# A batch pipeline with bf16 transposes, 8 KB loads of four consecutive rows, and a PSUM copy that restores the row order

## The chip, the cores and the metric

The kernel runs on one core of a Trainium2 chip. The metric is device time in microseconds, the median of several runs. A profile covers one execution; its span is some 2 us shorter than the timed figure (98.6 against 100.73 us for the kernel before). A run over 1.5% above the fastest of the same kernel counts as slow, and ratios use fast runs alone.

## The reference

```python
batch, m, k, n = 16, 512, 512, 512            # x: (16,512,512) fp32, weight: (512,512) fp32
y = scale * np.matmul(x, weight)              # scale = 0.125
y = np.where(mask == 1, y, -1e9)              # mask: strictly lower triangle
y_exp = np.exp(y - np.max(y, axis=-1, keepdims=True))
return y_exp / np.sum(y_exp, axis=-1, keepdims=True)
```

The mask is causal: rows 128·mt to 128·mt+127 need only the first 128·(mt+1) columns. Every kernel here uses that, so a tile of 128 output rows must hold consecutive rows. x is read (16.8 MB), the result written (16.8 MB).

## The kernel before

An item is 128 rows of one batch, 64 items in all. x is loaded one batch (1 MB) at a time with 2 KB rows, transposed in fp32 on PE, cast to bf16 on the way out of PSUM, multiplied, exponentiated with a row sum, and scaled.

```python
xf_pool = tile_pool(name="xf", bufs=3)                       # three batches of x
out_pool = tile_pool(name="outp", bufs=4)
x_r = x.rearrange("b (mt p) k -> b p mt k", p=P)             # 2 KB runs
out_r = out.rearrange("b (mt p) n -> b p mt n", p=P)

def stage_transpose(i):
    for kt in range(KT):
        nc.tensor.transpose(pxt[:, kt], xf[:, mt, kt*P:(kt+1)*P], ident_f32)

def stage_evict(i):
    nc.vector.tensor_copy(xt[:, :half], pxt[:, :half])       # fp32 PSUM -> bf16 SBUF
    nc.scalar.copy(xt[:, half:], pxt[:, half:])

# stage_matmul: 4 matmuls of (mt+1)*128 columns and one that adds the mask; ...
# stage_exp: nc.scalar.activation(Exp, accum_out=rsum); ...

def stage_norm(i):
    nc.vector.reciprocal(rinv, st_sum[i])
    nc.vector.tensor_scalar_mul(ot[:, mt, :NC], ot[:, mt, :NC], rinv)
    nc.gpsimd.memset(ot[:, mt, NC:], 0.0)                    # each batch anew
# ... loads issued from SP, stores from ACT
```

The softmax here doesn't subtract the row's maximum and nothing guards it: scores larger than these inputs give would overflow.

## Time and profile before

| | before |
|---|---|
| time, median | 100.73 us (100.1 to 100.77) |
| span of the profile | 98.6 us |
| bytes moved | 34.97 MB |
| GB/s from 30 to 84 us | 407 |
| busy: PE, DVE, ACT | 80%, 57%, 51% |

The prediction shows the lines of this profile. In short: in the middle of the span the transfers run at a flat 407 GB/s, so bytes set the pace; at both ends they don't.

### The profile page before, as it was taken

How to read it: one execution, taken by the hardware profiler on the slowest of the kernel's cores; microseconds unless marked ns; L12 is line 12 of the kernel's file. 1: busy time of each engine (PE TensorE's matmuls, PEld its weight loads, DVE VectorE, ACT ScalarE, POOL GpSimd, SP SyncE). 2: the span in 40 equal slices, each digit the busy share in tenths (PEclk: the TensorE clock that was granted, in tenths of full speed). 3: DMA queues.
4: the chain of work that ended last, by engine and by line, in shares of the span. 5: the costliest groups of instructions: out<-in, count | busy, mean ns of one | idle time of the engine just before them, and what ended most of it. 6: DMA issues, size and time to landing. Idle time of an engine off the chain costs nothing.

```text
span 98.6 us, 1837 instructions
## 1 busy us (share of the span) xinstructions
PE 79.1 (80%) x568; PEld 51.3 (52%) x576; DVE 56.4 (57%) x200; ACT 50.5 (51%) x193; POOL 23.4 (24%) x72
## 2 busy tenths in 40 slices
PE   0046499999999799999999998989898989898200
PEld 0045276756666556474655565656464656465000
DVE  0003826868685549595939394857566666657400
ACT  5000436656666545666747474647484848475400
POOL 7200023223120504141503132221404050502000
PEclk9999999999999999999999999999999999999996
DMA  0998995998999999999999999999999999974683
GB/s 27 315 405 269 404 367 152 367 315 265 401 405 407 407 410 404 405 410 400 411 407 409 406 411 405 401 408 408 410 404 410 410 403 405 395 292 175 256 301 125
DMA packets 18009, 34.97 MB, mean 355 GB/s; under 512 B 592, under 2 KB 1104, under 8 KB 18000
## 3 DMA queue, kind: packets, MB, share of 16 engines
q1 hardware_dynamic: 9552, 18.09, 49.1%
q10 hardware_dynamic: 8448, 16.78, 44.9%
q8 instruction: 4, 0.07, 0.2%
q14 instruction: 5, 0.04, 0.1%
HBM read 18.09 MB, written 16.78 MB: 354 GB/s over the span
## 4 chain that ended last, share of the span: by engine, by line
DMA 50%; PE 31%; DVE 8%; issue 2%; ACT 2%; SPq 0%; ACTq 0%
DMA xf<-in_x_dram 43%; PE py L118 16%; PE pxt L99 13%; DMA w_f<-in_weight_dram 8%; DVE xt L108 4%; DVE ot L159 2%; PE py L125 2%; DVE w_bf L54 1%; ACT ot L143 1%; ACT xt L109 1%; DVE rinv L158 1%; DVE diag_mask L61 1%; SPq L91 0%; ACTq L166 0%; ACTq L109 0%
## 5 line engine op out<-in xcount | busy, mean ns | idle before, releaser
L118 PE MATMUL py<-w_bf,xt 128*128 128x384 bf16 (+3 forms) x248 | 53.0, 306 | 4.1 <-DVE xt L108 2.3
L99 PE MATMUL pxt<-ident_f,xf 128*128 128x128 f32 x256 | 45.6, 284 | 8.6 <-DMA xf<-in_x_dram 8.6
L143 ACT ACTIVATE ot<-py 128x128 f32<-128x128 f32 (+1 forms) x64 | 28.0, 444 | 20.4 <-PE py L125 20.4
L99 PEld LDWEIGHTS pxt<-ident_f,xf 128*128 128x128 f32 x256 | 29.1, 146 | 15.6 <-issue 6.4
L109 ACT CAST xt<-pxt 128x256 bf16<-128x256 f32 x64 | 23.7, 370 | 20.8 <-DVE xt L108 9.4
L108 DVE CAST xt<-pxt 128x256 bf16<-128x256 f32 x64 | 26.8, 420 | 8.8 <-PE pxt L99 8.8
L118 PEld LDWEIGHTS <-xt 128*128 128x128 bf16 x256 | 18.1, 99 | 21.3 <-DVE xt L108 14.7
L159 DVE TENSOR_SCALAR ot<-ot,rinv 128x128 f32<-128x128 f32 (+1 forms) x64 | 25.8, 403 | 3.4 <-POOL ot L161 0.5
L161 POOL MEMSET ot<- 128x384 f32 (+2 forms) x48 | 14.3, 336 | 38.0 <-DMA out_dram<-ot 38.0
L158 DVE RECIPROCAL rinv<-rsum 128x1 f32<-128x1 f32 x64 | 10.0, 156 | 15.7 <-ACT ot L143 15.7
L163 POOL MEMSET ot<- 1x512 f32 x16 | 8.3, 516 | 28.6 <-DVE ot L159 28.3
L125 PE MATMUL py<-diag_mask,ident_bf 128*128 128x128 bf16 x64 | 14.2, 222 | 0.0
L143 ACT ACTIVATION_READ_ACCUMULATOR ot<-py 128x1 f32 x64 | 13.2, 206 | 0.0
L125 PEld LDWEIGHTS <-ident_bf 128*128 128x128 bf16 x64 | 6.4, 100 | 3.3 <-issue 0.2
L54 DVE CAST w_bf<-w_f 128x512 bf16<-128x512 f32 x4 | 1.4, 422 | 8.9 <-DMA w_f<-in_weight_dram 8.9
L109 ACT ACT_TABLE_LOAD x1 | 1.3, 1283 | 0.7 <-PEq L202 0.7
L61 DVE TENSOR_SCALAR diag_mask<-diag_mask_f 128x128 bf16<-128x128 f32 x4 | 0.7, 220 | 0.0
masks.py:199 POOL TENSOR_SCALAR_AFFINE_SELECT ident_f<-ident_f 128x128 f32<-128x128 f32 x1 | 0.3, 297 | 0.0
masks.py:199 POOL TENSOR_SCALAR_AFFINE_SELECT ident_bf<-ident_bf 128x128 bf16<-128x128 bf16 x1 | 0.3, 297 | 0.0
masks.py:197 POOL MEMSET ident_f<- 128x128 f32 x1 | 0.2, 205 | 0.3 <-POOLq L202 0.3
masks.py:197 POOL MEMSET ident_bf<- 128x128 bf16 x1 | 0.2, 207 | 0.0
L202 POOL MEMSET const-float32-0.0<- 128x1 f32 x1 | 0.1, 104 | 0.2 <-issue 0.2
(3 smaller groups left out, 0.3 us busy)
## 6 DMA issues: line engine op xcount, KB each, us to landing
xf<-in_x_dram SPq DMA_DIRECT2D x16, 1024.0 KB, 10.5
out_dram<-ot ACTq DMA_DIRECT2D x16, 1024.0 KB, 9.7
w_f<-in_weight_dram SPq DMA_DIRECT2D x1, 1024.0 KB, 7.6
diag_mask_f<-in_mask_dram SPq DMA_DIRECT2D x4, 64.0 KB, 7.3
```

What stands on the lines that cost most here:

```text
L54: nc.vector.tensor_copy(w_bf[:, kt], w_f32[:, kt])
L61: nc.vector.tensor_scalar(out=diag_mask[:, mt], in0=diag_mask_f32[:, mt], scalar1=-MASK_NEG, scalar2=MASK_NEG, op0=mybir.AluOpType.mult, o ...
L99: nc.tensor.transpose(pxt[:, kt], xf[:, mt, kt * P : (kt + 1) * P], ident_f32)
L108: nc.vector.tensor_copy(xt[:, :half], pxt[:, :half])
L109: nc.scalar.copy(xt[:, half:], pxt[:, half:])
L118: nc.tensor.matmul(py[:, :NC], lhsT=xt[:, kt], rhs=w_bf[:, kt, :NC], start=(kt == 0), stop=(kt == KT - 1),)
L125: nc.tensor.matmul(py[:, mt * P : NC], lhsT=ident_bf, rhs=diag_mask[:, mt], start=False, stop=True, skip_group_check=True,)
L143: nc.scalar.activation(out=ot[:, mt, :NC], in_=st_py[i][:, :NC], func=AF.Exp, bias=0.0, scale=float(scale), accum_out=rsum,)
L158: nc.vector.reciprocal(rinv, st_sum[i])
L159: nc.vector.tensor_scalar_mul(ot[:, mt, :NC], ot[:, mt, :NC], rinv)
L161: nc.gpsimd.memset(ot[:, mt, NC:], 0.0)
L163: nc.gpsimd.memset(ot[0:1, 0, :], 1.0 / N)
```

## The change

Its intent: fetch x earlier (eight buffers in place of three, all loads queued at once) and with longer runs (each partition takes four consecutive rows, 8 KB); transpose in bf16 (on PE four fp32 transposes take 0.45 us in the trace of before, four bf16 matmuls of the same width 0.22); use fewer and larger instructions; and write the zeros above the diagonal once. A partition p now holds rows 4p to 4p+3, so a transpose yields columns in the order (t, p) and the copy out of PSUM must put them back to 4p+t: it reads straight and writes bf16 elements four apart.

```diff
+X_BUFS = 8
+OUT_BUFS = 6
-    x_r = x.rearrange("b (mt p) k -> b p mt k", p=P)
+    x_r = x.rearrange("b (p t) k -> b p t k", t=MT)
...
+    def prepare(b):
+        nc.vector.tensor_copy(xb, xf)                        # cast 128x2048 to bf16
+        for h in range(2):
+            pt = psum_t.tile([P, 2, M], BF16, name="pt")
+            for kk in range(2):
+                for mt in range(MT):
+                    nc.tensor.transpose(pt[:, kk, mt*P:(mt+1)*P], xb[:, mt, kt*P:(kt+1)*P], ident_bf)
+            src = pt.rearrange("k c (t p) -> k c t p", p=P)
+            dst = xt[:, 2*h:2*h+2].rearrange("k c (p t) -> k c t p", t=MT)
+            if h == 0: nc.vector.tensor_copy(dst, src)
+            else:      nc.scalar.copy(dst, src)
...
+    # multiply(b): the matmuls and exponentials of four row tiles, as before
+    # normalise(b): one reciprocal of 128x4, four scalings; store(b) from SP
+    for b in range(B):
+        if b + 1 < B:
+            prepare(b + 1)
+        multiply(b)
+        normalise(b)
+        store(b)
+        if b + X_BUFS < B:
+            load(b + X_BUFS)
```

The kernel's text has no waits; the program builder puts them in and fixes the order of the instructions on each engine, which need not be that of the source (in the trace of before DVE runs two casts in a row, at 44.08 and 44.74 us, where the source alternates one cast with one scaling).

More of the change, by code (lines that the diff above doesn't have):

```diff
@@ L12 @@
 AF = mybir.ActivationFunctionType
+ALU = mybir.AluOpType
 MASK_NEG = -512.0
+P = 128
+X_BUFS = 8
+OUT_BUFS = 6
 @with_exitstack
@@ L30 @@
     K2, N = weight.shape
-    assert K == K2
-    P = 128
+    assert K == K2 and N == 512 and K == 512 and M == 512
     MT = M // P
     KT = K // P
-    assert N == 512 and K == 512 and M == 512
     const = ctx.enter_context(tc.tile_pool(name="const", bufs=1))
-    setup = ctx.enter_context(tc.tile_pool(name="setup", bufs=1))
-    ident_f32 = const.tile([P, P], FP32)
-    make_identity(nc, ident_f32)
-    ident_bf = const.tile([P, P], BF16)
-    make_identity(nc, ident_bf)
-    w_f32 = setup.tile([P, KT, N], FP32)
@@ L47 @@
-    w_bf = const.tile([P, KT, N], BF16)
-    diag_mask = const.tile([P, MT, P], BF16)
-    diag_mask_f32 = setup.tile([P, MT, P], FP32)
-    def stage_setup():
-        nc.sync.dma_start(w_f32, weight.rearrange("(kt p) n -> p kt n", p=P))
-        for kt in range(KT):
-            nc.vector.tensor_copy(w_bf[:, kt], w_f32[:, kt])
-        for mt in range(MT):
-            nc.sync.dma_start(
-                diag_mask_f32[:, mt],
-                mask[mt * P : (mt + 1) * P, mt * P : (mt + 1) * P],
-            )
-            nc.vector.tensor_scalar(
-                out=diag_mask[:, mt],
-                in0=diag_mask_f32[:, mt],
-                scalar1=-MASK_NEG,
-                scalar2=MASK_NEG,
-                op0=mybir.AluOpType.mult,
-                op1=mybir.AluOpType.add,
-            )
@@ L70 @@
-    xf_pool = ctx.enter_context(tc.tile_pool(name="xf", bufs=3))
-    xt_pool = ctx.enter_context(tc.tile_pool(name="xt", bufs=4))
-    out_pool = ctx.enter_context(tc.tile_pool(name="outp", bufs=4))
-    sum_pool = ctx.enter_context(tc.tile_pool(name="sums", bufs=8))
-    psum_t = ctx.enter_context(tc.tile_pool(name="psum_t", bufs=3, space=bass.MemoryType.PSUM))
-    psum_y = ctx.enter_context(tc.tile_pool(name="psum_y", bufs=4, space=bass.MemoryType.PSUM))
-    n_items = B * MT
-    st_xf = [None] * (B + 1)
@@ L79 @@
-    st_pxt = [None] * n_items
-    st_xt = [None] * n_items
-    st_py = [None] * n_items
-    st_ot = [None] * (B + 1)
-    st_sum = [None] * n_items
-    st_rinv = [None] * n_items
-    x_r = x.rearrange("b (mt p) k -> b p mt k", p=P)
-    out_r = out.rearrange("b (mt p) n -> b p mt n", p=P)
-    def stage_load(b):
-        xf = xf_pool.tile([P, MT, K], FP32, name="xf")
-        nc.sync.dma_start(xf, x_r[b])
-        st_xf[b] = xf
-    def stage_transpose(i):
-        b, mt = divmod(i, MT)
-        xf = st_xf[b]
-        pxt = psum_t.tile([P, KT, P], FP32, name="pxt")
-        for kt in range(KT):
-            nc.tensor.transpose(
-                pxt[:, kt], xf[:, mt, kt * P : (kt + 1) * P], ident_f32
-            )
-        st_pxt[i] = pxt
@@ L104, in stage_evict @@
-    def stage_evict(i):
-        pxt = st_pxt[i]
-        xt = xt_pool.tile([P, KT, P], BF16, name="xt")
-        half = KT // 2
-        nc.vector.tensor_copy(xt[:, :half], pxt[:, :half])
-        nc.scalar.copy(xt[:, half:], pxt[:, half:])
-        st_xt[i] = xt
-    def stage_matmul(i):
-        b, mt = divmod(i, MT)
-        NC = (mt + 1) * P
-        xt = st_xt[i]
-        py = psum_y.tile([P, N], FP32, name="py")
-        for kt in range(KT):
-            nc.tensor.matmul(
-                py[:, :NC],
-                lhsT=xt[:, kt],
-                rhs=w_bf[:, kt, :NC],
-                start=(kt == 0),
-                stop=(kt == KT - 1),
-            )
-        nc.tensor.matmul(
-            py[:, mt * P : NC],
-            lhsT=ident_bf,
-            rhs=diag_mask[:, mt],
-            start=False,
-            stop=True,
-            skip_group_check=True,
-        )
-        st_py[i] = py
@@ L135, in stage_exp @@
-    def stage_exp(i):
-        b, mt = divmod(i, MT)
-        NC = (mt + 1) * P
-        if mt == 0:
-            ot = out_pool.tile([P, MT, N], FP32, name="ot")
-            st_ot[b] = ot
-        ot = st_ot[b]
-        rsum = sum_pool.tile([P, 1], FP32, name="rsum")
-        nc.scalar.activation(
-            out=ot[:, mt, :NC],
-            in_=st_py[i][:, :NC],
-            func=AF.Exp,
-            bias=0.0,
-            scale=float(scale),
-            accum_out=rsum,
-        )
-        st_sum[i] = rsum
@@ L153, in stage_norm @@
-    def stage_norm(i):
-        b, mt = divmod(i, MT)
-        NC = (mt + 1) * P
-        ot = st_ot[b]
-        rinv = sum_pool.tile([P, 1], FP32, name="rinv")
-        nc.vector.reciprocal(rinv, st_sum[i])
-        nc.vector.tensor_scalar_mul(ot[:, mt, :NC], ot[:, mt, :NC], rinv)
-        if NC < N:
-            nc.gpsimd.memset(ot[:, mt, NC:], 0.0)
-        if mt == 0:
-            nc.gpsimd.memset(ot[0:1, 0, :], 1.0 / N)
-    def stage_store(b):
-        nc.scalar.dma_start(out_r[b], st_ot[b])
@@ L168 @@
-    for it in range(n_items + 3):
-        if it == 0:
-            stage_load(0)
-            stage_setup()
-        if it < n_items:
-            b, mt = divmod(it, MT)
-            if mt == 0 and b > 0:
-                stage_load(b)
-            stage_transpose(it)
-        if 1 <= it <= n_items:
-            stage_evict(it - 1)
-            stage_matmul(it - 1)
-        if 2 <= it <= n_items + 1:
-            stage_exp(it - 2)
-        if 3 <= it <= n_items + 2:
-            stage_norm(it - 3)
-            if (it - 3) % MT == MT - 1:
-                stage_store((it - 3) // MT)
+    x_pool = ctx.enter_context(tc.tile_pool(name="xf", bufs=X_BUFS))
@@ new lines @@
+    xb_pool = ctx.enter_context(tc.tile_pool(name="xb", bufs=2))
+    xt_pool = ctx.enter_context(tc.tile_pool(name="xt", bufs=2))
+    sum_pool = ctx.enter_context(tc.tile_pool(name="sums", bufs=4))
+    psum_t = ctx.enter_context(tc.tile_pool(name="psum_t", bufs=4, space=bass.MemoryType.PSUM))
+    psum_y = ctx.enter_context(tc.tile_pool(name="psum_y", bufs=4, space=bass.MemoryType.PSUM))
+    x_r = x.rearrange("b (p t) k -> b p t k", t=MT)
+    out_r = out.rearrange("b (mt p) n -> b p mt n", p=P)
@@ new lines, with load @@
+    ident_bf = const.tile([P, P], BF16, name="ident_bf")
+    w_f32 = const.tile([P, KT, N], FP32, name="w_f32")
+    w_bf = const.tile([P, KT, N], BF16, name="w_bf")
+    diag_f32 = const.tile([P, MT, P], FP32, name="diag_f32")
+    diag_bf = const.tile([P, MT, P], BF16, name="diag_bf")
+    ots = [const.tile([P, MT, N], FP32, name=f"ot{i}") for i in range(OUT_BUFS)]
+    st_x, st_xt, st_py, st_sum = {}, {}, {}, {}
+    def load(b):
+        xf = x_pool.tile([P, MT, K], FP32, name="xf")
+        nc.sync.dma_start(xf, x_r[b])
+        st_x[b] = xf
@@ new lines, in prepare @@
+    def prepare(b):
+        xf = st_x.pop(b)
+        xb = xb_pool.tile([P, MT, K], BF16, name="xb")
+        nc.vector.tensor_copy(xb, xf)
+        xt = xt_pool.tile([P, KT, M], BF16, name="xt")
+        for h in range(2):
+            pt = psum_t.tile([P, 2, M], BF16, name="pt")
+            for kk in range(2):
+                kt = 2 * h + kk
+                for mt in range(MT):
+                    nc.tensor.transpose(
+                        pt[:, kk, mt * P : (mt + 1) * P],
+                        xb[:, mt, kt * P : (kt + 1) * P],
+                        ident_bf,
+                    )
+            src = pt.rearrange("k c (t p) -> k c t p", p=P)
+            dst = xt[:, 2 * h : 2 * h + 2].rearrange("k c (p t) -> k c t p", t=MT)
+            if h == 0:
+                nc.vector.tensor_copy(dst, src)
+            else:
+                nc.scalar.copy(dst, src)
+        st_xt[b] = xt
@@ new lines, in multiply @@
+    def multiply(b):
+        xt = st_xt.pop(b)
+        ot = ots[b % OUT_BUFS]
+        rsum = sum_pool.tile([P, MT], FP32, name="rsum")
+        for mt in range(MT):
+            NC = (mt + 1) * P
+            py = psum_y.tile([P, N], FP32, name="py")
+            for kt in range(KT):
+                nc.tensor.matmul(
+                    py[:, :NC],
+                    lhsT=xt[:, kt, mt * P : NC],
+                    rhs=w_bf[:, kt, :NC],
+                    start=(kt == 0),
+                    stop=(kt == KT - 1),
+                )
+            nc.tensor.matmul(
+                py[:, mt * P : NC],
+                lhsT=ident_bf,
+                rhs=diag_bf[:, mt],
+                start=False,
+                stop=True,
+                skip_group_check=True,
+            )
+            nc.scalar.activation(
+                out=ot[:, mt, :NC],
+                in_=py[:, :NC],
+                func=AF.Exp,
+                bias=0.0,
+                scale=float(scale),
+                accum_out=rsum[:, mt : mt + 1],
+            )
+        st_sum[b] = rsum
@@ new lines, in normalise, with store @@
+    def normalise(b):
+        ot = ots[b % OUT_BUFS]
+        rinv = sum_pool.tile([P, MT], FP32, name="rinv")
+        nc.vector.reciprocal(rinv, st_sum.pop(b))
+        for mt in range(MT):
+            NC = (mt + 1) * P
+            nc.vector.tensor_scalar_mul(ot[:, mt, :NC], ot[:, mt, :NC], rinv[:, mt : mt + 1])
+        nc.gpsimd.memset(ot[0:1, 0, :P], 1.0 / N)
+    def store(b):
+        nc.sync.dma_start(out_r[b], ots[b % OUT_BUFS])
+    load(0)
+    nc.sync.dma_start(w_f32, weight.rearrange("(kt p) n -> p kt n", p=P))
@@ new lines @@
+    for mt in range(MT):
+        nc.sync.dma_start(diag_f32[:, mt], mask[mt * P : (mt + 1) * P, mt * P : (mt + 1) * P])
+    for b in range(1, X_BUFS):
+        load(b)
+    make_identity(nc, ident_bf)
+    for ot in ots:
+        for mt in range(MT - 1):
+            nc.gpsimd.memset(ot[:, mt, (mt + 1) * P :], 0.0)
+        nc.gpsimd.memset(ot[0:1, 0, P:], 1.0 / N)
+    prepare(0)
+    for kt in range(KT):
+        if kt % 2 == 0:
+            nc.vector.tensor_copy(w_bf[:, kt], w_f32[:, kt])
+        else:
+            nc.scalar.copy(w_bf[:, kt], w_f32[:, kt])
@@ L189 @@
+    nc.vector.tensor_scalar(
+        out=diag_bf,
+        in0=diag_f32,
+        scalar1=-MASK_NEG,
+        scalar2=MASK_NEG,
+        op0=ALU.mult,
+        op1=ALU.add,
+    )
+    for b in range(B):
[6 more added lines that the diff above has]
+            load(b + X_BUFS)
 _INS = ['x', 'weight', 'scale', 'mask']
```

## The prediction

> **What bounds the kernel now.** I read the page's slices first, because they show when a resource is full and not only how full it is on average; then windows of the plateau and of both ends; then the waits; last the groups of instructions, for durations.
>
> ```profile
> PE   0046499999999799999999998989898989898200
> DVE  0003826868685549595939394857566666657400
> DMA  0998995998999999999999999999999999974683
> GB/s 27 315 405 269 404 367 152 367 315 265 401 405 407 407 410 404 405 410 400 411 407 409 406 411 405 401 408 408 410 404 410 410 403 405 395 292 175 256 301 125
> ...
> q1 hardware_dynamic: 9552, 18.09, 49.1%
> q10 hardware_dynamic: 8448, 16.78, 44.9%
> ```
>
> A slice is 2.465 us. In most of the span the GB/s row is flat near 407: there, bytes set the pace. The q lines (packets, MB, share) show that a packet is about 2 KB and that loads (q1) and stores (q10) are nearly all of the bytes.
>
> ```profile
> 30.00:84.00 54.00, 50.66 (x377) 32.09 (x381) 35.49 (x127) 32.55 (x128) 14.41 (x40) 1.00 1.05 407
> ...
> 2.00:3.00 1.00, 0.00 (x0) 0.00 (x0) 0.00 (x0) 0.02 (x1) 1.00 (x6) 1.00 0.71 102
> 3.00:4.00 1.00, 0.00 (x0) 0.00 (x0) 0.00 (x0) 0.00 (x0) 0.17 (x2) 1.00 0.88 342
> ...
> 97.00:98.00 1.00, 0.00 (x0) 0.00 (x0) 0.00 (x0) 0.00 (x0) 0.00 (x0) 0.50 0.01 2
> ```
>
> These are windows: busy us of PE, weight loads, DVE, ACT, POOL; clock; DMA share; GB/s. On the plateau a batch moves 1.049 MB in and 1.049 MB out: 2.097 MB / 407 GB/s = 5.15 us. PE looks full too (50.7 of 54), but its matmul ends are modelled and the rate that stands still is the DMA's.
>
> Outside the plateau bytes are lost. All 34.97 MB at 407 GB/s are 85.9 us, so 12.7 us of the 98.6 are lost. Slices 0 to 11 sum to 3692 against 12 x 407 = 4884, so 1192/407 x 2.465 = 7.2 us are lost there; the last five sum to 1149 against 2035, 5.4 us. Two parts stay in any version of this kind: by 4.0 us 0.47 MB have moved, worth 1.15 us, so the flow starts in effect at 2.85 us; and 1.6 us pass from the last bytes at 97.0 to the end. The rest can be won: 7.2 - 2.85 = 4.35 us at the start and 5.4 - 1.6 = 3.8 us at the end, together 8.1 us.
>
> ```profile
> SPq L91 <- PE pxt L99: 62.3, 13, 8.4
> ...
> POOL ot L161 <- DMA out_dram<-ot: 38.0, 11, 3.8
> ```
>
> The waits say why the start is lost: with three x buffers the fourth load waits until the transposes free one (13 waits, 62.3 us in the queue). While PE catches up with the 9 us late weight, nothing is queued. At the end only stores are left and they come at the compute's pace.
>
> [...] The trace sits at 407, so 2 KB take 16 x 2048 / 407 = 80.5 ns on an engine[...]. [...]loads alone (405 in slice 2) and loads with stores (407) do run equally fast here. [...]512 elements from SBUF take 422 ns, 256 from PSUM 420. [...]bf16 written with a stride of four is 8 bytes[...]. No run here shows that case.
>
> **The change part by part**, from these groups:
>
> ```profile
> L54 DVE CAST w_bf<-w_f 128x512 bf16<-128x512 f32 x4 | 1.4, 422 | 8.9 <-DMA w_f<-in_weight_dram 8.9
> L108 DVE CAST xt<-pxt 128x256 bf16<-128x256 f32 x64 | 26.8, 420 | 8.8 <-PE pxt L99 8.8
> L109 ACT CAST xt<-pxt 128x256 bf16<-128x256 f32 x64 | 23.7, 370 | 20.8 <-DVE xt L108 9.4 <-DVE rinv L158 6.1 <-POOL ot L161 5.1
> L158 DVE RECIPROCAL rinv<-rsum 128x1 f32<-128x1 f32 x64 | 10.0, 156 | 15.7 <-ACT ot L143 15.7
> L143 ACT ACTIVATE ot<-py 128x512 f32<-128x512 f32 x16 | 9.8, 610 | 0.3 <-PE py L125 0.3
> ```
>
> DVE, per batch. Removed: four PSUM casts, 4 x 0.42 = 1.68, and three of four reciprocals, 0.47. Added: a cast of 2048 elements to bf16. [...] Added: one strided PSUM copy of 1024 elements[...]. Kept: the four scalings, 0.29 + 0.35 + 0.42 + 0.48 = 1.54 in the plateau, and one reciprocal, 0.16. Sum 4.14 us, against 3.85 now by the same durations.
>
> ACT, per batch. Four copies (4 x 0.37 = 1.48) become one of 1024 elements: the exponentials give (610-286)/384 = 0.84 ns an element, so 0.86 + 0.16 = 1.02. The exponentials with their accumulator reads occupy 0.34 + 0.36 + 0.48 + 0.58 = 1.76 by their starts in the timeline. Sum 2.8 us.
>
> PE, per batch. The chain shows four fp32 transposes in 0.45 us and four bf16 matmuls of the same width in 0.22. Sixteen transposes go from 1.8 to about 0.9 us. [...] Sum 3.3 us.
>
> So DVE at 4.14, PE at 3.3 and ACT at 2.8 all lie beside the 5.15 us of the bytes. On the plateau, halving the transposes is worth nothing by itself.
>
> Loads. Eight x buffers put 9.7 MB in the queue at once, 24 us of transfer, and the first store, at 18.3 us before, should come by about 15. I therefore count the 4.35 us as won, less 0.5 for a hole. Stores then share the queue behind the loads. At the end, compute runs ahead of the bytes and the six output tiles hold a backlog, so the last stores go back to back: 3.8 us won if the last batch is finished 1.6 + 2.6 us before the end. With batch 0 done at 15 us and an end at 90, this allows (85.8-15)/15 = 4.7 us a batch; 4.14 fits with 0.6 to spare.
>
> Descriptors. If the 8 KB stay one packet, four packets become one[...].
>
> POOL. Zeros are written once, no longer per batch; its 38.0 us of waiting for stores and its hold on DVE go, both off the path.
>
> Sum: 98.6 - 3.85 - 3.8 - 1.0 = 89.95 us of span. The timed median is 2.1 us over the span (100.73 - 98.6), so about **92 us**; I put 91.7.
>
> **The rivals.**
>
> One: a serial loop. In source order the next batch's cast, transposes and copy stand ahead of this batch's exponentials and scalings. Followed strictly, a round is 1.2 + 0.9 + 1.0 + 1.8 + 0.2 + 1.5 plus handovers of about 0.3 = 6.9 us, and 15 x 6.9 + 15 + 4 = 122 us. Against it: the instruction order in the trace is not that of the source, which alternates one cast with one scaling, while DVE ran
>
> ```profile
> 42.68 0.70 DVE L159 TENSOR_SCALAR ot<-ot,rinv 128x512 f32<-128x512 f32 x1
> 43.30 0.41 DVE L108 CAST xt<-pxt 128x256 bf16<-128x256 f32 x1
> ...
> 44.08 0.42 DVE L108 CAST xt<-pxt 128x256 bf16<-128x256 f32 x1
> 44.74 0.42 DVE L108 CAST xt<-pxt 128x256 bf16<-128x256 f32 x1 [0.24 <-PE pxt L99]
> ```
>
> two casts in a row. Instructions are ordered by readiness when the program is built, and I expect that here.
>
> Two: DVE becomes the bound. If the strided write halves the copy's rate, it takes 2.3 us, DVE 5.2 a batch, and the end is 15 + 15 x 5.2 + 4.2 + 2.1 = 99 us: the same as now. Waits of 0.6 us a batch on a cast or a row sum do a milder form of it, 93 to 96 us.
>
> Three: the one queue. A store issued behind seven loads lands up to 18 us later; six output tiles give about 6 x 4.3 = 26 us, so this holds narrowly. If not, compute stalls, but the queue is full meanwhile; cost 0 to 2 us.
>
> [...]
>
> **Range and chances.** [...] Small holes and the mild form of rival two reach up. The range is 89.5 to 97.5. Faster by over 2% means below 98.7: 0.87. Within 2%, mostly rival two: 0.08. Slower, mostly rival one: 0.05.
>
> **What would show it.** Right: GB/s flat from the second slice to the last but one[...]; about 128 packets per x load; no wait of the load queue on PE; DVE near 66 us busy with few idle stretches; transposes about half of 45.6 us busy; both new copies near 1.2 and 1.0 us. Wrong: a GB/s row below 400 in mid-span with DVE at 9 (rival two) or with no engine above 7 and DVE, PE and ACT waiting on one another (rival one); packets still 2 KB (no descriptor gain); stores arriving singly at the end.

The sums came to 98.6 - 3.85 - 3.8 - 1.0 = 89.95 us of span, about 92 us with the 2.1 us of the timed median. The 1.0 us in it is half of an estimated 2.0 us for the 8 KB loads, and the byte floor from the trace's 407 GB/s alone is 92.4 us (2.85 + 85.9 + 1.6 + 2.1). DVE's 4.14 us a batch has 1.22 us each for the cast and the strided copy; PE's 3.3 has 2.1 us for the matmuls and 0.3 for the masks. These were estimates, at rates that were not shown; so are the figures that build on them, the 6.9 us of rival one, the 2.3 and 5.2 us of rival two and the 66 us of DVE.

## The result, and the profile after

| | before | after |
|---|---|---|
| time, median of 4 | 100.75 us (100.1 to 100.94) | 125.33 us (124.04 to 127.08); the two fast runs 124.1 |
| span of the profile | 98.6 us | 122.3 us |
| GB/s, 30 to 54 us | about 407 | 416 |
| GB/s, 58 to 112 us | about 407 (to 84) | 189 |

The kernel became slower: the ratio is 1.234 (95% interval 1.226 to 1.241). A ratio is the mean time of one kernel's fast runs over that of the other's of the same rounds, so not quite the ratio of the medians; two of the four runs of after, at 126.5 and 127.1, count as slow.

From the page of the changed kernel, the slices (3.06 us each) and the two groups of the new copy:

```profile
DVE  0159449789999999968727667387474872764400
ACT  4019195689798799391570933907519157097200
DMA  3999999999999999999999808027063090440872
GB/s 86 366 309 420 426 429 423 426 394 396 410 437 408 414 424 394 432 413 408 435 396 420 335 21 311 31 82 261 0 236 112 5 338 0 159 184 0 312 263 111
...
L93 ACT COPY xt<-pt 128x1024 bf16<-128x1024 bf16 x16 | 38.9, 2430 | 33.6 <-issue 30.7
L91 DVE COPY xt<-pt 128x1024 bf16<-128x1024 bf16 x16 | 38.7, 2421 | 5.8 <-PE pt L82 5.8
```

There are two things to see. The GB/s row has two halves: full up to about 68 us, as predicted, then in pieces. The compute slows down sooner, from about 50 us; the loads already in the queue keep the transfers full for a while. The last load is issued at 57.6 us, and once it has landed only stores are left, one for each round of the compute. And one copy takes 2.42 us on either engine, where the prediction had put 1.22 (estimate) and 1.02. In the second half no engine is near 9 throughout, so no engine is full: they wait for one another. A round is the work of one batch, from one cast to the next. One round of the second half, from the timeline of after (start, duration, engine, instruction, and in brackets how long the engine sat idle before):

```profile
55.67 1.03 PE L104 MATMUL py<-w_bf,xt 128*128 128x512 bf16 x4
...
57.00 1.21 DVE L75 CAST xb<-xf 128x2048 bf16<-128x2048 f32 x1
...
58.27 1.07 PE L82 MATMUL pt<-ident_bf,xb 128*128 128x128 bf16 x16 [1.51 <-DVE xb L75]
58.93 2.42 DVE L91 COPY xt<-pt 128x1024 bf16<-128x1024 bf16 x1 [0.71 <-PE pt L82]
59.42 2.42 ACT L93 COPY xt<-pt 128x1024 bf16<-128x1024 bf16 x1 [3.93 <-issue]
...
61.58 0.36 ACT L119 ACTIVATE ot<-py 128x128 f32<-128x128 f32 x1
...
63.47 0.18 DVE L132 RECIPROCAL rinv<-rsum 128x4 f32<-128x4 f32 x1 [2.12 <-ACT ot L119]
...
63.74 1.29 DVE L135 TENSOR_SCALAR ot<-ot,rinv 128x128 f32<-128x128 f32 x4
...
64.95 1.22 DVE L75 CAST xb<-xf 128x2048 bf16<-128x2048 f32 x1
```

The matmuls of a batch are done by 56.8 us (their last, the mask's, starts at 56.54), and ACT is free from about 55.5. It does not start that batch's exponentials before 61.58: its next instruction in order is the copy of the *following* batch, for which it sits idle 3.93 us. That copy waits for transposes, these for the cast on DVE, and the cast stands behind the scalings of the batch before. So the round closes: cast 1.27, transposes 0.66 to the first copy, 0.49 to ACT's copy, that copy 2.16, exponentials 1.89, reciprocal and scalings 1.48 (all by starts). The sum is 7.95 us, and the starts of the cast, 57.00 and 64.95, lie 7.95 apart. ACT's wait before its copy appears as "issue", which means that the profile saw no event to name. That it is a wait for the transposes is read from the timeline: they end at 59.34 us and the copy starts at 59.42.

The granted clock is not the cause. It fell towards the end of this round, to 0.70 from 62 to 64 us and 0.50 from 64 to 66, but the round before, from 49.04 to 57.00 us, ran at 1.00 and took as long, 7.96 us.

In the first half the order is another one, in which ACT puts the copy between two pairs of exponentials, and DVE goes copy, cast, reciprocal, scalings without a gap. There a round takes 4.80 us (casts at 29.97, 34.78 and 39.58), with DVE busy 23.84 of 24 us (30 to 54):

```profile
29.97 1.25 DVE L75 CAST xb<-xf 128x2048 bf16<-128x2048 f32 x1
...
32.56 2.41 DVE L91 COPY xt<-pt 128x1024 bf16<-128x1024 bf16 x1
34.78 1.24 DVE L75 CAST xb<-xf 128x2048 bf16<-128x2048 f32 x1
```

The order of ACT as built, which the trace follows, shows where it turns (first number: place; Activation is an exponential, TensorCopy the copy; after ot5 comes ot0 again):

```
30 Activation ot5 128x128      35 TensorCopy  xt (batch 7)     40 TensorCopy  xt (batch 8)
31 Activation ot5 128x256      36 Activation ot0 128x128       41 Activation ot1 128x128
32 TensorCopy  xt (batch 6)    37 Activation ot0 128x256       42 Activation ot1 128x256
33 Activation ot5 128x384      38 Activation ot0 128x384       ...
34 Activation ot5 128x512      39 Activation ot0 128x512
```

### The profile page after: what moved, and what is told of

Same layout as the page of the kernel before. It is cut to its first block, busy times and chain, and to the rows that moved or that the text cites. A ratio compares the mean times of both kernels' runs of the same rounds, so it can differ in the third digit from the quotient of the medians.

```text
span 122.3 us, 1597 instructions
## 1 busy us (share of the span) xinstructions
PE 66.6 (54%) x568; PEld 44.7 (37%) x576; DVE 80.4 (66%) x115; ACT 67.6 (55%) x147; POOL 14.0 (11%) x46
## 2 busy tenths in 40 slices
DMA packets 11862, 34.95 MB, mean 286 GB/s; under 512 B 592, under 2 KB 1104, under 8 KB 9808
## 5 line engine op out<-in xcount | busy, mean ns | idle before, releaser
L93 ACT COPY xt<-pt 128x1024 bf16<-128x1024 bf16 x16 | 38.9, 2430 | 33.6 <-issue 30.7
L91 DVE COPY xt<-pt 128x1024 bf16<-128x1024 bf16 x16 | 38.7, 2421 | 5.8 <-PE pt L82 5.8
L104 PEld LDWEIGHTS <-xt 128*128 128x128 bf16 x256 | 24.0, 109 | 47.7 <-DVE xt L91 32.4
L82 PE MATMUL pt<-ident_bf,xb 128*128 128x128 bf16 x256 | 17.8, 225 | 12.9 <-DVE xb L75 12.7
L75 DVE CAST xb<-xf 128x2048 bf16<-128x2048 f32 x16 | 20.0, 1247 | 5.8 <-DMA xf<-in_x_dram 5.8
L82 PEld LDWEIGHTS <-xb 128*128 128x128 bf16 x256 | 15.4, 101 | 16.7 <-DVE xb L75 16.4
L135 DVE TENSOR_SCALAR ot<-ot,rinv 128x128 f32<-128x128 f32 (+1 forms) x64 | 20.7, 384 | 1.1
L136 POOL MEMSET ot<- 1x128 f32 x16 | 5.5, 341 | 101.3 <-DVE ot L135 101.3
L111 PE MATMUL py<-diag_bf,ident_bf 128*128 128x128 bf16 x64 | 15.5, 242 | 0.0
L152 POOL MEMSET ot<- 128x384 f32 (+2 forms) x18 | 6.0, 364 | 0.0
```

The costliest lines, as they stand in the source:

```text
L75: nc.vector.tensor_copy(xb, xf)
L82: nc.tensor.transpose(pt[:, kk, mt * P : (mt + 1) * P], xb[:, mt, kt * P : (kt + 1) * P], ident_bf,)
L91: nc.vector.tensor_copy(dst, src)
L93: nc.scalar.copy(dst, src)
L104: nc.tensor.matmul(py[:, :NC], lhsT=xt[:, kt, mt * P : NC], rhs=w_bf[:, kt, :NC], start=(kt == 0), stop=(kt == KT - 1),)
L111: nc.tensor.matmul(py[:, mt * P : NC], lhsT=ident_bf, rhs=diag_bf[:, mt], start=False, stop=True, skip_group_check=True,)
```

## The experiments

Theory: two causes make each other worse. The strided write makes each copy slow, and the order of the second half puts the copy, with three other steps, on a loop that nothing overlaps. Rivals: the stride alone; the order alone; or a third cause, such as stores queued behind loads in one queue or the six output tiles.

The diffs below are shortened; lines with words in place of code describe longer edits. The experiments ran in three sessions on three chips, with the kernel before at 100.6 to 100.73 us in each; a ratio is to before in the same session. Where the text says that one kernel beats another, every run of the one was below every run of the other.

### Straight copy, order as built

```diff
-    x_r = x.rearrange("b (p t) k -> b p t k", t=MT)
+    x_r = x.rearrange("b (t p) k -> b p t k", p=P)           # 2 KB runs again
-            src = pt.rearrange(...); dst = xt[...].rearrange(...)
+            src = pt;                dst = xt[:, 2*h:2*h+2]
```

> The changed kernel with one part undone: x is loaded as 2 KB rows as before, so the PSUM copy is straight on both sides and the result stays right. It separates the cost of the strided copy from the rest. If the stride is what doubled the copies (2.42 us on both engines), they now take about 1.2 us on DVE and 1.0 us on ACT; if bf16 in PSUM or the longer copy is the cause, they stay above 2 us. The issue order of the second half is as in the changed kernel (next batch's copy ahead of this batch's exponentials), so the serial-loop theory expects rounds of 7.95 - 1.4 = 6.5 us from the sixth batch on and about 103 us in all; a theory in which the stride alone explains the loss expects 91 to 94 us.

Measured: 103.37 us, ratio 1.034 (1.020 to 1.048), result correct. Its groups of the copy:

```profile
L93 ACT COPY xt<-pt 128x1024 bf16<-128x1024 bf16 x16 | 16.2, 1012 | 36.8 <-issue 31.2 <-ACT ot L119 3.3 <-PE pt L82 2.3
L91 DVE COPY xt<-pt 128x1024 bf16<-128x1024 bf16 x16 | 11.0, 685 | 5.8 <-PE pt L82 5.7
```

So neither bf16 in PSUM nor the length makes the copy slow: straight, it takes 0.69 us on DVE, less than the 1.2 expected, and 1.01 on ACT. The idle time of ACT before its copy is still there (31.2 us), and reciprocals in the second half start 6.63 us apart (57.19, 63.81, 70.44). The serial loop stands without the stride, so the stride alone does not explain the loss.

### A first attempt to hold the order

```diff
+    # order edges: same engine, no wait
+    after(copy_on_ACT(b), last_exponential(b - 1))
+    after(reciprocal(b), cast(b + 2))
+    # source: cast(b+2); multiply(b); prepare(b+1); normalise(b)
```

> The changed kernel with the strided copy kept, but the issue order held by explicit order edges (no waits): ACT does the four exponentials of a batch ahead of the next batch's copy, and DVE the cast two batches ahead before this batch's row sums. Serial-loop theory: the 7.95 us rounds of the second half become DVE-bound rounds of about 5.0 us (2.42 + 1.22 + 1.5), span near 96 us, time 97 to 101. Rival (the stride alone, or stores queued behind loads, sets the second half): still 115 us or more.

Measured: 119.2 us, 116.67 to 127.27; the profiled run is slow, at a granted clock of 0.679. The expected 97 to 101 us failed: even the one fast run took 116.67, where the rival had 115 or more. It does not decide between the two, since the edit made a loop of its own. In the waits of this slow profile DVE's copy stands for the transposes, and the weight loads of the matmuls for the copy:

```profile
DVE xt L104 <- PE pt L95: 25.6, 11, 3.5
...
PEld L119 <- DVE xt L104: 20.0, 9, 3.2
```

In source order all matmuls of a batch now came ahead of the next batch's transposes, and the matmuls wait for the copy: copy, matmuls, transposes, copy. Holding two engines in order is not enough if the third closes the ring.

### Both undone

```diff
+    straight copy and 2 KB runs (first experiment) and the edges of the second
```

> Both undone at once: straight copy from 2 KB rows and the pinned order. If stride and order are the whole loss, DVE needs some 3.9 us a batch, ACT 2.8, and the bytes set the pace as the prediction had it: GB/s flat near 407 and 91 to 94 us. If something third costs time (one queue for loads and stores, six output tiles), it stays above 97.

Measured: 95.95 us, ratio 0.957 (0.948 to 0.966). The same edges that looped with the long copy do little harm with the short one, and the bytes set the pace:

```profile
GB/s 27 293 403 280 381 402 386 389 385 388 386 390 404 407 407 398 409 407 404 407 412 397 409 410 409 407 410 408 403 409 409 406 407 409 409 409 409 409 239 7
```

It stayed 2 us above the expected 91 to 94: loads alone with 2 KB runs reach only some 387 GB/s (slices 4 to 11 of 2.34 us), less than the 405 that one slice of before had suggested. One queue and six output tiles were kept, so neither is needed to explain the loss.

### Twelve output tiles

```diff
-OUT_BUFS = 6
+OUT_BUFS = 12
```

> One constant changed: 12 output tiles in place of 6, all else as in the changed kernel. The issue order as built switches to copy-before-exponentials exactly where the first output tile is used again (batch 6); with 12 tiles the built order does the exponentials of a batch before the next batch's copy from the seventh batch to the last. If re-use of the output tiles is what turned the order, the 7.95 us rounds vanish: rounds near 5 us, 98 to 104 us in all, with copies still 2.42 us. If the number of x buffers or a true wait on stores on the chip is the cause, nothing changes: about 125 us.

Measured: 118.55 us, 115.37 to 121.7; the profiled run is slow, so only its order is read here, not its time. The built order did move: the long run of rounds with the copy directly ahead of a whole set of exponentials, from batch 6 on, is gone, and from batch 8 on ACT does a batch's exponentials and then the next copy. But PE then had the transposes behind all matmuls, which is the loop of the second experiment, and rounds took 6.9 us (reciprocals at 83.27, 90.09 and 96.98). The expectation of rounds near 5 us failed. Re-use of the output tiles thus changes where the builder turns the order; that it is the only reason is not shown.

### The order of the first half for all batches

```diff
+    # ACT: exp 0, exp 1, copy(b+1), exp 2, exp 3     PE: matmuls 0, 1, transposes(b+1), matmuls 3
+    # DVE: copy(b+1), cast(b+2), reciprocal(b), scalings(b)
+    after(copy_on_ACT(b + 1), exponential(b, 1));  after(exponential(b, 2), copy_on_ACT(b + 1))
+    after(transposes(b + 1), matmuls(b, 1));       after(matmuls(b, 3), transposes(b + 1))
+    after(cast(b + 2), copy_on_DVE(b + 1));        after(reciprocal(b), cast(b + 2))
```

> Strided copy kept; the issue order of the changed kernel's own first half (period 4.8 us, DVE full) is held for all batches by order edges: on ACT two exponentials, the next batch's copy, two exponentials; on PE the transposes of the next batch between this batch's matmuls; on DVE copy, next cast, reciprocal, scalings. The earlier attempt to hold the order (116 to 127 us) put the transposes behind all matmuls and so made another serial loop through PE. Theory: with the order alone repaired, rounds are 4.8 to 5.1 us to the end, span about 16.8 + 15 x 5.0 + 5 = 96 to 98, time 97 to 101 us. If it stays above 110, the strided copy alone makes the second half slow.

Measured: 100.94 us, ratio 1.012 (1.000 to 1.025), result correct. With the strided copy kept and only the order repaired, a kernel of 124 us (fast runs) takes 101. DVE is full to the end and sets the pace; its timeline:

```profile
65.46 2.42 DVE L110 COPY xt<-pt 128x1024 bf16<-128x1024 bf16 x1
67.67 1.25 DVE L84 CAST xb<-xf 128x2048 bf16<-128x2048 f32 x1
69.15 0.18 DVE L159 RECIPROCAL rinv<-rsum 128x4 f32<-128x4 f32 x1 [0.23 <-ACT ot L145]
69.42 1.29 DVE L164 TENSOR_SCALAR ot<-ot,rinv 128x128 f32<-128x128 f32 x4
70.64 2.41 DVE L110 COPY xt<-pt 128x1024 bf16<-128x1024 bf16 x1
```

From copy to copy is 5.18 us here and 4.84 to 4.87 in every other round, about what the bytes of a batch need (5.15 us at the 407 GB/s of before). This is rival two of the prediction, which put it at 99 us.

### The stride moved to the reading side

```diff
-            src = pt.rearrange("k c (t p) -> k c t p", p=P)
-            dst = xt[...].rearrange("k c (p t) -> k c t p", t=MT)
+            src = pt.rearrange("k c (t p) -> k c p t", p=P)
+            dst = xt[...].rearrange("k c (p t) -> k c p t", t=MT)
```

The order edges of the run before are kept.

> As the run with the first half's order, but the copy reads PSUM with the stride and writes SBUF straight (same result). If the 2.42 us come from writes that are 8 bytes apart in SBUF, the copies fall to between 0.7 and 1.2 us on DVE and 1.0 on ACT, DVE needs some 3.6 us a batch and the kernel becomes bound by its bytes, 92 to 96 us. If any stride on either side costs as much, copies stay at 2.4 us and the time near that of the run before.

Measured: 93.2 us (93.09 to 93.64), ratio 0.935 (0.924 to 0.947), result correct. This kernel beats both.

```profile
GB/s 43 355 318 301 407 427 430 423 423 423 416 403 423 410 411 439 379 438 401 429 399 433 401 426 407 411 439 395 431 402 404 408 408 408 408 410 409 407 193 6
...
L110 DVE COPY xt<-pt 128x1024 bf16<-128x1024 bf16 x16 | 19.4, 1212 | 1.1 <-PE pt L98 1.1
L112 ACT COPY xt<-pt 128x1024 bf16<-128x1024 bf16 x16 | 16.2, 1012 | 9.5 <-ACT ot L145 5.5 <-issue 2.2 <-PE pt L98 1.8
```

The elements moved are the same, in another order: reading PSUM 256 bytes apart and writing SBUF straight takes 1.21 us on DVE and 1.01 on ACT, which are the predicted 1.22 and 1.02. On ACT the read-side stride costs nothing against the straight copy; on DVE it takes 1.21 us in place of 0.69. All the surplus of the 2.42 us over the prediction is in the strided write.

### Stride two

```diff
-    x_r = x.rearrange("b (p t) k -> b p t k", t=MT)
+    x_r = x.rearrange("b (h p t) k -> b p h t k", h=2, t=2)   # two rows, 4 KB; write stride two
```

> Two consecutive rows to a partition (4 KB runs) in place of four, so that the copy writes bf16 with a stride of two, 4 bytes. [...]the copies fall clearly below 2.42 us, to about 1.2 on both engines, and the time to 92 to 96 us. If any step but one loses the rate, they stay at 2.4 us and the time stays near 98.

What the run decides is whether the cost falls with the stride, or is the same for any.

Measured: 93.68 us, ratio 0.939 (0.928 to 0.951), result correct, with the held order.

```profile
L112 ACT COPY xt<-pt 128x1024 bf16<-128x1024 bf16 x16 | 20.8, 1301 | 9.9 <-ACT ot L145 6.9 <-PE pt L98 1.8 <-issue 1.1
L110 DVE COPY xt<-pt 128x1024 bf16<-128x1024 bf16 x16 | 20.6, 1288 | 1.1 <-PE pt L98 1.1
```

Both engines again take nearly the same time. Without a fixed part of some 155 ns (an estimate, from the 156 ns that a reciprocal of 128x1 takes on DVE in the trace of before), 1024 elements take 2.27 us with stride four and 1.14 us with stride two: 2.2 and 1.1 ns an element. The elements of a pass lie 8 bytes apart and then 4, so that is 0.28 ns for each byte walked over in both cases. In these two cases the cost followed the span of memory walked over, not the elements written. The evidence for stride two is ACT's: 1.30 us against 1.01 for a straight write. DVE's 1.29 is hardly above the 1.21 of its copy with a strided read, and says less. Why both engines meet the same figure was not tried.

### What the 8 KB loads are worth

```diff
+    the changed kernel with a straight copy (rows come out in the wrong order, on purpose)
+    and the edges of the second experiment
```

> Wrong result on purpose: 8 KB loads kept, but the copy is straight, so rows come out in the wrong order; order edges as in the 95.95 us run with 2 KB rows and straight copy. It differs from that run only in how x is loaded and so shows what the 8 KB runs are worth[...]. Expected 93 to 95 us, against 95.95; loads alone at 425 GB/s in the first 25 us, where 2 KB rows gave 386. If descriptors' size is worth nothing, 96 us again.

Measured: 93.02 us, against 95.95 of the same kernel with 2 KB runs (the run with both undone). The ratio to the kernel before is 0.933 (0.918 to 0.948). The result is wrong. And a correct pair in the held order of the first half, with 2 KB runs and a straight copy:

```diff
+    straight copy and 2 KB runs with the edges of the 100.94 us run
```

> 2 KB rows, straight copy and the order of the first half held, so that it differs from the 93.2 us run (8 KB rows, read-side stride) in the x loads and in a cheaper copy. If the 8 KB loads are worth the 2 us of the prediction, this takes 95 to 96.5 us; if the copy's side mattered, less than 93.

Measured: 95.85 us, ratio 0.951 (0.945 to 0.958), against 93.2 with 8 KB runs.

```profile
GB/s 27 345 404 219 368 405 387 387 387 386 388 387 406 409 407 397 408 409 400 410 403 406 409 408 410 407 409 408 401 407 408 408 409 407 407 411 407 409 206 7
```

Compare slices 6 to 11 with those of the 93.2 us run: 387 against some 420 GB/s while loads run alone. In both pairs the 8 KB loads are worth 2.7 to 2.9 us, though in the second the copy differs as well (0.68 against 1.21 us on DVE, off the path).

### The one-line edit alone

```diff
+    stride on the reading side; order as built
```

> The changed kernel with the stride moved from the write to the read side of the copy and nothing else; the issue order as built is the serial one from the sixth batch on. Copies 1.21 and 1.01 us as in the run with the held order. Two-cause theory: serial rounds of 7.95 - 1.4 = 6.55 us remain in the second half, as in the run with straight copies and 2 KB rows (6.63), and the time is 101 to 105 us. If the cheap copy alone repairs the kernel, 93 to 95 us and no wait of ACT before its copy.

Measured: 104.91 us, ratio 1.041 (1.030 to 1.052). Copies take 1.21 and 1.01 us, and the serial rounds remain, 6.63 us between most reciprocals of the second half (58.36, 64.99, 71.62):

```profile
L93 ACT COPY xt<-pt 128x1024 bf16<-128x1024 bf16 x16 | 16.2, 1012 | 34.4 <-issue 31.2
...
58.36 0.18 DVE L132 RECIPROCAL rinv<-rsum 128x4 f32<-128x4 f32 x1 [1.99 <-ACT ot L119]
...
64.99 0.18 DVE L132 RECIPROCAL rinv<-rsum 128x4 f32<-128x4 f32 x1 [1.99 <-ACT ot L119]
```

A cheap copy alone does not repair the kernel; it still loses to the kernel before.

### The cast taken out of the loop

```diff
+    after(reciprocal(b), cast(b + 2))      # one edge; strided write and ACT's order kept
```

> The changed kernel with the strided write, and one edge only: DVE's cast runs two batches ahead, before this batch's reciprocal; ACT keeps its copy ahead of the exponentials. If the loop closes through DVE's cast (scalings, cast, transposes, copy, exponentials, scalings), taking the cast out of it shortens the round by 1.2 + 0.7 us to about 6 us or less: 104 to 112 us. If ACT's order alone makes the loop, rounds stay at 7.95 us and the time near 125.

Measured: 114.95 us, ratio 1.139 (1.127 to 1.150). Expected were 104 to 112, or 125: it lies between. Of seven slow rounds four are 6.27 us and three 7.5 to 7.95 (reciprocals at 76.53, 82.80, 90.30, 96.58). The cast was indeed on the loop. What is left in the trace is a loop through PE: ACT's copy stands ahead of the exponentials, the next batch's matmuls wait for the first exponential (2.74 us idle at 81.41), and behind the matmuls stand the transposes that the following copy needs. In the three longer rounds the matmuls ran at a lower granted clock (0.67 from 61 to 65 us, 0.76 to 0.82 from 65 to 73, 0.63 from 81.3 to 85.1): 3.7 us at 0.63, against 2.5 us at 1.00 (88.9 to 91.4) in a round of 6.28.

The four corners, with 8 KB loads throughout (fast runs):

| | order as built | order of the first half held |
|---|---|---|
| strided write, 2.42 us | 124.1 us | 100.9 us |
| strided read, 1.21 and 1.01 us | 104.9 us | 93.2 us |

## Why the prediction was wrong, point by point

**The bound and the ends: right.** Once both causes are gone, the kernel does what the sum said: GB/s is flat from near the start to the end, and 93.2 us lies in the range, 1.5 us above the point. That it lies so near is in part luck: the sum had 1.0 us for the 8 KB loads, which were worth 2.7 to 2.9, so its other terms came out some 3 us too low. Of this about 1.8 us is at the end: in the 93.2 us run the transfers fall off at 87.0 us, and the bytes moved after that are worth 0.9 us at 407 GB/s, so 3.5 us remain to the end at 91.4, where 1.6 were kept. The 8 KB loads came as one packet for each partition (9,808 of the 11,862 packets are under 8 KB; the other 2,054 are about 128 for each of 16 loads), ran at 420 to 429 GB/s alone in the changed kernel, and were worth more than the estimated 2.0 us of which the prediction took half; that estimate set out from 407 for 2 KB loads, which was too high when they run alone (387), and its rate for the 8 KB was not shown.

**Failed step one: "one strided PSUM copy of 1024 elements", put at 1.22 us.** It measured 2.42 us, and ACT's 2.43 in place of 1.02. The 1.22 was the estimate, at a rate that was not shown; that a write with a stride of four keeps such a rate was assumed, with the note "No run here shows that case". The runs show that it does not: stride four took 2.42 us, stride two 1.29. By itself, with a good order, this step costs 100.9 - 93.2 = 7.7 us and makes DVE the bound: rival two.

**Failed step two: "Instructions are ordered by readiness when the program is built, and I expect that here".** It held for the first six batches (0 to 5) and not after. The evidence offered, an order in the trace of before that differs from the source, shows only that the builder reorders, not that it reorders well. After the first pass over the output tiles the built order has the next batch's copy ahead of exponentials whose inputs, in the round shown, had been ready for 4.8 us or more (56.8 to 61.58). Why the builder chose it is not shown. By itself, with a cheap copy, this costs 104.9 - 93.2 = 11.7 us: rival one, given 5%. Its round was put at 6.9 us and measured 6.63 in the two runs with cheap copies.

**Together: 124.1 - 93.2 = 30.9 us, 11.5 more than 7.7 + 11.7.** Off the loop, ACT's copy overlaps with other work. On the loop its surplus of 1.4 us is paid each round: the seven rounds of the second half took 55.7 us with the slow copy and 47.5 with the cheap one (six of 6.63 and one of 7.66), 8.2 us more. The remaining 3 us were not traced.

**Rival one's total was close by accident.** 122 us assumed 15 rounds of 6.9; the kernel had seven of 7.95 after a first half of 4.8.

**Side terms.** The transposes fell to 17.8 us busy from 45.6, with 16 in 1.07 us where about 0.9 was predicted, worth nothing here. DVE was put at 66 us busy and had 80.4: the 1.2 us of each copy, sixteen times, less 4 us that the scalings took less than predicted (20.7 against 24.6), and overlaps count once. Three terms came without a trace; measured were 1.25 us for the cast and 1.21 for the copy with a strided read (both put at 1.22), and for the matmuls and masks of a batch 2.4 us by their starts (54.12 to 56.54 in the trace of after; put at 2.1 and 0.3), in which four matmuls of 512 columns take 0.87. The sum gave 92.05; the 91.7 that was put has no working. Rival three, the one queue, was small: in the 93.2 us run ACT waited 9.0 us for stores to free output tiles without lengthening the end, since transfers ran throughout.

What stays open: why the builder turns the order just there. Re-use of output tiles takes part (twelve tiles moved the turn), but no run isolates it.

## What to carry to other kernels

Ask of each engine's instruction order whether an instruction that waits on a long chain stands ahead of work that is ready; an idle engine just before such an instruction, with "issue" as the reason and no engine full, is the sign, and the sum of one round's steps is the check. When a layout must be permuted on the way out of PSUM, try the stride on the read and a straight write: here this took 1.21 and 1.01 us in place of 2.42. Where a rate for an unusual access pattern carries the argument, price the case in which it is wrong and see whether it also makes another rival worse: here the two together cost 11.5 us more than the sum of their single costs.
